# A two-layer hybrid diffusion block: six buffers for the first modulation weights, and the state space model's input without its repeated part in DRAM

## The chip, the cores and the metric

The kernel runs on one core of a Trainium2 chip. The metric is the device time of one execution in microseconds (us); less is better. A time shown for a kernel is the median of several executions; the profile is of one execution more.

## The reference, cut to what matters

Context (256 tokens) and latent (512 tokens) pass through the same two layers. Width is 1024, everything is fp32. A layer modulates the normed tokens by six vectors that come from one product of a 1024-vector with a 1024x6144 matrix, projects them once for four mixers, joins these by one output projection, and ends in a gated ConvFFN.

```python
for l in range(DEPTH):
    m = silu(c) @ ada_w + ada_b + ada_table[l]          # shift, scale, gate, twice
    h = modulate(rmsnorm(x, g0), shift1, scale1)
    p = h @ w_in[l]                                     # 256 + 768 + 1024 + 352 columns
    y = concat(s5(p), hyena(p), retention(p), mla(p)) @ w_out[l]
    x = x + gate1 * rmsnorm(y, g1)
    h = modulate(rmsnorm(x, g2), shift2, scale2)
    y = (silu(a) * v) @ w_down[l]                       # a, v: depthwise conv of h @ w_up[l]
    x = x + gate2 * rmsnorm(y, g3)

def s5(u):                       # 16 groups of 16 channels, 64 complex states each
    h_f = scan(abar_f, bbar_f @ u); h_b = scan(abar_b, bbar_b @ u reversed)
    y = gelu(Re(C_f h_f + C_b h_b) + d_skip * u)
    return y * sigmoid(y @ glu_w + glu_b)
```

The first block of modulation vectors (a 1024x2048 matrix: shift and scale of the first norm of the first layer) is needed before anything can be projected. The backward scan of the latent tokens starts from the state that the context leaves behind; this is why its input holds the context's part at both ends.

## The kernel before, in words

The work is written as generators (the mixers of a layer, preparations of tables, modulation blocks), woven together by the program and then put in one order for each engine (TensorE PE, VectorE DVE, ScalarE ACT, GpSimd POOL, and SP, which issues most transfers) by a scheduler. Each engine runs its own list in order. A product is done in three passes: a weight tile of 128x1024 (512 KB, pool names `wr` raw, `wh` and `wl`) is loaded, cast by ACT (L303) to its high part, DVE subtracts it to get the low part (L304), and PE multiplies high by high, low by high and high by low (L335, L339).

**The start** (L1676 to L1711). Three tiles of x, each of 1024 channels by 256 tokens (1 MB, two transfers, L1686), are loaded, then a loop walks the letters of `W_START`: `x` does the norm of the next x tile (`xnorm`, L1691: ACT squares L1502, PE sums them over channels L1481, a root on DVE L402 to L408, PE spreads it L423, DVE multiplies L1695), `p` runs a step of `s5_prep` (tables of the state space model), `s` a step of `hy_spectra` (the Hyena filters), and `a` a step of `ada(0)` (L463): step k loads two tiles of the modulation matrix (L473, buffer name `ar`, three buffers that every such product shares) and multiplies them by the vector (L478, four matmuls). After eight steps the row is copied (L481), transposed (L484), added to its bias (`mod`, L488) and turned into the norm's gain (`der`, L497). Then `norm_half` (L1526) scales x on ACT (L1530) and DVE (L1528) and splits it into high and low parts (`H1h`, L1531, ACT; `H1l`, L1532, DVE; H1 is the latent tokens, H0 the context). With these the in-projection of the first layer begins.

**The state space model.** `s5_in` (L957) projects its 256 input channels first and stores each half (128 channels, 8 phases j, 96 chunks n) into the DRAM tile `s5_u`, whose rows have 128 places per phase: the 96 chunks (L967) and once more the first 32, which are the context's (L968). `s5_run` (L970) loads that into a tile U with phases and channels in the partitions (L977, eight transfers, one per phase) and its kernel T (L978, eight transfers), alternating, all on POOL's queue. `states` (L981) multiplies U by the input matrices (L995: forward columns 0 to 95, backward columns 127 down to 32), DVE rotates and scans (L1002 to L1016); the outputs are L1027 to L1035. At the end u is loaded once more for the skip term (L1061). In the same queue POOL copies the roots of a retention norm (into a tile also named `A_SB`, L1235, behind a wait for DVE), starts transfers of the latent attention's operands (B_Q and B_R, L1365; `wh` and `wl` from `B_kr`, L1367) and clears A_HS (L1011), all in one list in order.

**The second layer's** in-projection comes in the order state space, Hyena, retention, MLA; the retention's values are made last by `ip_v` (L1742; weights `w_v`, matmuls L1749 to L1751), and `s5_run` and the rest are woven in behind.

Of the kernel before, what the change touches and what calls it, by code (L numbers as in the profile page):

```python
# [19 lines left out]
L = 2  # L20
# [3 lines left out]
KD = D // 128  # L24
# [3 lines left out]
NCH = NT // 8  # L28
# [12 lines left out]
QUEUES = "ssssassssp"  # L41
W_START = "xaxapxsapasapasaaa"
TLS = False
# [182 lines left out]
def tile_kernel(ctx, tc, I, out, dbg=None, upto=None):  # L226
# [9 lines left out]
    def new(p, shape, tag, dt=F32, **kw):  # L236
        return p.tile(list(shape), dt, tag=tag, name=nm(tag), **kw)
# [195 lines left out]
    def dtile(shape, tag):  # L433
        return new(dr, shape, tag)
# [7 lines left out]
    hy_Kc = dtile([2, 2, 128, 768], "hy_Kc")  # L442
    s5_u = [dtile([256, 8, 128], f"s5_u{l}") for l in range(L)]
    s5_y = [dtile([256, 8, NCH], f"s5_y{l}") for l in range(L)]
# [20 lines left out]
    def ada(b):  # L465

        md, der = mods[0]
        ps = sm_ps()
        for k in range(KD):
            raws = []  # L470
            for h in range(2):
                raw = new(wp, [128, 1024], "ar", bufs=3)
                qa.dma_start(raw, I["ada_w"][b, k, h])  # L473
                raws.append(raw)
            for h in range(2):
                for j in range(2):
                    q = 32 * (2 * h + j)
                    pe.matmul(ps[q:q + 32], c2[:, k], raws[h][:, j * 512:(j + 1) * 512], start=(k == 0), stop=(k == KD - 1))  # L478
            yield
        row = new(wp, [128, 512], "ar", bufs=3)  # L480
# [478 lines left out]
    def s5_in(l, inproj):  # L959
        for i in range(2):  # L960
# [4 lines left out]
            act.copy(tv[:, 0:32], o[0].rearrange("p (n j) -> p n j", j=8))  # L965
            u = s5_u[l][128 * i:128 * i + 128]
            qs.dma_start(u[:, :, 0:96], t)  # L967
            qs.dma_start(u[:, :, 96:128], t[:, :, 0:32])  # L968

    def s5_run(l, p, put, segs, busy=lambda: False):  # L970
        ud, yd = s5_u[l].rearrange("(g c) j n -> j c g n", c=16), s5_y[l].rearrange("(g c) j n -> j c g n", c=16)
        n0 = 0 if 0 in segs else 32
# [3 lines left out]
        for j in range(8):  # L976
            qp.dma_start(U[16 * j:16 * j + 16], ud[j])  # L977
            qp.dma_start(T[16 * j:16 * j + 16].rearrange("c g (i x) -> c g i x", i=8), s5_T[l][:, :, j:j + 8, :])  # L978
        tt = dve.tensor_tensor

# [77 lines left out]
        for i in range(2):  # L1058
            tu = new(p, [128, 2, 8, NCH], ("A_U", "A_T")[i])
            t, u = tu[:, 0], tu[:, 1]  # L1060
            qc.dma_start(u[:, :, n0:], s5_u[l][128 * i:128 * i + 128][:, :, n0:96])  # L1061
            qc.dma_start(t[:, :, n0:], s5_y[l][128 * i:128 * i + 128][:, :, n0:])
# [552 lines left out]
    for l in range(L):  # L1615
# [48 lines left out]
        with ExitStack() as base, ExitStack() as esl, ExitStack() as esr:  # L1664
# [5 lines left out]
            if l == 0:  # L1670
# [9 lines left out]
                with mkpool("start", side="right") as px:  # L1680
                    g0 = ada(0)
                    X = []
                    for i, (s, h) in enumerate(subs):
# [4 lines left out]
                        if i == 0:  # L1688
                            c2 = ada_setup()

                    def xnorm(x):  # L1691
# [337 lines left out]
```

## Time and profile before

| | us |
|---|---|
| median of 3 runs | 2100.9 (2097.35 to 2101.09) |
| the profiled execution | 2094.68 |
| its span, from the first to the last instruction | 2092.9 |

| engine | busy us | share of the span |
|---|---|---|
| PE, matmuls | 1917.5 | 92% |
| PE, weight loads | 1563.2 | 75% |
| DVE | 1350.6 | 65% |
| ACT | 796.8 | 38% |
| POOL | 136.8 | 7% |

The mean granted clock of PE is 0.948 of full speed. The span has these parts: the start (0 to 68.9 us), the first layer's in-projection with the tables woven in (to 340), its mixers and output projection (to 600), its ConvFFN (to 1345, with the second layer's in-projection behind it to about 1430), the mixers of the second layer (to 1720) and the last ConvFFN. A stretch in which PE is busy for less than its length is one where something else ends last.

### The profile page before, as it was taken

To read this page: it belongs to the slowest core of one execution; us is meant where nothing else is said; L and a number is where in the kernel's file an instruction comes from. 1 tells how busy PE (TensorE), PEld (TensorE's weight loads), DVE (VectorE), ACT (ScalarE), POOL (GpSimd) and SP (SyncE) were. 2 spreads that over 40 slices of the span, in tenths; PEclk is the share of its full clock that TensorE was granted. 3 is DMA by queue.
4 is the path that set the end of the run, shared out by engine and by line. 5 is a ranking of instruction groups with operands and counts; after the bars stand their busy time and mean duration, and the time that the engine had idled before them with its cause. 6 is when DMAs were issued, how large, how long until landed. Compare 5 with 4: busy or idle time off the path is not lost. (4 is left out here: it accounts for less than half of the span.)

```text
span 2092.9 us, 29826 instructions
## 1 busy us (share of the span) xinstructions
PE 1917.5 (92%) x11318; PEld 1563.2 (75%) x11318; DVE 1350.6 (65%) x2850; ACT 796.8 (38%) x1355; POOL 136.8 (7%) x158
## 2 busy tenths in 40 slices
PE   5899899787899799899999999889989989999996
PEld 1677676566688678788888888678867878888885
DVE  5777474686746897876856445738877455555555
ACT  3656222343334332343533233423355434333332
POOL 0121002100001000110000000110021000000000
PEclk7899999789999899999999999899989989999998
DMA  7566446625442468234133222395631424232231
GB/s 254 178 215 219 172 147 195 155 78 165 149 163 91 154 208 283 92 104 143 59 97 139 86 63 69 104 227 170 219 106 53 137 74 132 92 100 96 96 101 41
DMA packets 147127, 283.96 MB, mean 136 GB/s; under 512 B 35397, under 2 KB 78566, under 8 KB 146984
## 3 DMA queue, kind: packets, MB, share of 16 engines
q1 hardware_dynamic: 139304, 273.65, 40.5%
q0 software_dynamic: 3072, 7.08, 2.0%
q10 hardware_dynamic: 4608, 1.31, 0.3%
q8 instruction: 90, 1.47, 0.3%
q14 instruction: 53, 0.43, 0.1%
HBM read 230.12 MB, written 48.99 MB: 133 GB/s over the span
## 5 line engine op out<-in xcount | busy, mean ns | idle before, releaser
L304 DVE TENSOR_TENSOR wl<-wr,wh 128x1024 fp32r<-128x1024 f32 x174 | 213.3, 1228 | 277.7 <-ACT wh L303 273.9
L339 PE MATMUL mm<-H1h,wh 128*128 128x512 f32 x888 | 355.9, 401 | 14.4 <-DVE st L430 13.4
L339 PE MATMUL mm<-H1l,wh 128*128 128x512 f32 x888 | 353.9, 399 | 0.0
L339 PE MATMUL mm<-H1h,wl 128*128 128x512 f32 x888 | 353.4, 398 | 0.3 <-DVE wl L304 0.3
L303 ACT CAST wh<-wr 128x1024 fp32r<-128x1024 f32 x174 | 182.1, 1050 | 353.1 <-PE mm L339 288.0
L339 PEld LDWEIGHTS mm<-H1h,wh 128*128 128x128 f32 x888 | 169.1, 190 | 59.0 <-issue 17.0
L339 PEld LDWEIGHTS mm<-H1l,wh 128*128 128x128 f32 x888 | 169.4, 191 | 39.0 <-issue 3.2
L339 PEld LDWEIGHTS mm<-H1h,wl 128*128 128x128 f32 x888 | 169.0, 190 | 39.1 <-issue 2.0
L339 PE MATMUL mm<-H0h,wh 128*128 128x256 f32 x480 | 137.6, 287 | 9.6 <-DVE st L430 8.4
L339 PE MATMUL mm<-ff_mh,wh 128*128 128x512 f32 (+1 forms) x432 | 135.0, 363 | 8.4 <-DVE st L430 3.6
L339 PE MATMUL mm<-H0h,wl 128*128 128x256 f32 x480 | 137.2, 286 | 0.0
L339 PE MATMUL mm<-H0l,wh 128*128 128x256 f32 x480 | 136.9, 285 | 0.0
L339 PE MATMUL mm<-ff_ml,wh 128*128 128x512 f32 (+1 forms) x432 | 133.2, 359 | 0.0
L339 PE MATMUL mm<-ff_mh,wl 128*128 128x512 f32 (+1 forms) x432 | 132.8, 359 | 0.0
L339 PEld LDWEIGHTS mm<-H0h,wh 128*128 128x128 f32 x480 | 92.2, 192 | 17.3 <-issue 14.5
L339 PEld LDWEIGHTS mm<-H0h,wl 128*128 128x128 f32 x480 | 92.0, 192 | 4.6 <-issue 4.4
L339 PEld LDWEIGHTS mm<-H0l,wh 128*128 128x128 f32 x480 | 91.9, 192 | 3.2 <-issue 2.4
L1549 POOL TENSOR_TENSOR x<-x,y 128x512 f32<-128x512 f32 x20 | 28.4, 1426 | 994.6 <-ACT n_sq L1995 368.5
L1936 DVE TENSOR_TENSOR y<-mm,y 128x512 f32<-128x512 f32 x80 | 53.3, 686 | 59.4 <-PE mm L339 59.4
L339 PEld LDWEIGHTS mm<-ff_mh,wh 128*128 128x128 f32 x432 | 73.4, 192 | 23.6 <-DVE y L1936 5.1
L428 ACT ACTIVATE st<-mm,c_ffn_v 128x512 f32<-128x512 f32 (+1 forms) x132 | 88.6, 702 | 4.6 <-PE mm L354 4.6
L429 DVE SCALAR_TENSOR_TENSOR st<-mm,c_ffn_v,st 128x511 f32<-128x511 f32 (+1 forms) x132 | 83.4, 653 | 3.5 <-ACT st L428 3.5
(610 smaller groups left out, 4192.8 us busy)
## 6 DMA issues: line engine op xcount, KB each, us to landing
wr<-in_w_up SPq DMA_DIRECT2D x88, 512.0 KB, 3.6
ar<-in_ada_w SPq DMA_DIRECT2D x48, 512.0 KB, 4.6
ar<-in_ada_t SPq DMA_DIRECT2D x48, 512.0 KB, 4.4
wr<-in_w_down SPq DMA_DIRECT2D x44, 512.0 KB, 3.4
wr<-in_w_in SPq DMA_DIRECT2D x34, 512.0 KB, 4.5
ar<-in_k_tabl SPq DMA_DIRECT2D x16, 512.0 KB, 4.0
wr<-in_w_out SPq DMA_DIRECT2D x16, 512.0 KB, 4.6
xs_d<-x SPq DMA_DIRECT2D x8, 1024.0 KB, 5.0
```

Source lines behind the costliest of these rows:

```text
L303: act.copy(hi, raw)
L304: dve.tensor_tensor(lo, raw, hi.bitcast(F32), ALU.subtract)
L339: pe.matmul(outs[s], w, X(k, s, j), start=f, stop=z)
L428: act.activation(u[:, o:o + m], ps, AF.Identity, bias=vw[:, 3:4], scale=vw[:, 1:2])
L429: dve.scalar_tensor_tensor(u[:, o + 1:o + m], ps[:, 0:m - 1], vw[:, 0:1], u[:, o + 1:o + m], ALU.mult, ALU.add)
L1549: (pool, dve)[k // 2 % 2].tensor_tensor(x[:, ks], x[:, ks], y[:, ks], ALU.add)
L1936: dve.tensor_tensor(d, ps, d, ALU.add)
```

## The change

Four things are changed.

- `ada(0)` no longer shares three buffers: its two tiles of each step go to an `ar` and a `wr` buffer, three of each. Steps 0 to 2 are loaded when the first `run(g0, 1)` is made, which is behind the first x tile; each later step loads the tiles of the step three ahead. The later blocks of `ada` are as before.
- `W_START` has one `p` and one `s` less (these steps run later, in the in-projection), and `a` stands where they stood.
- `s5_u` holds 96 chunks per phase, with no repeated part; one transfer stores it, 3072 B in one piece per partition, where there were pieces of 384 B and 128 B. U is loaded into the first 96 columns in pieces of 384 B (512 B before), and POOL copies columns 0 to 31 to 96 to 127. The last reload of u takes the whole row.
- In `s5_run` the eight transfers of T are issued first, then the eight of U.

```diff
--- before.py
+++ after.py
@@ -39,7 +39,7 @@
 REUSE = "pool"
 
 QUEUES = "ssssassssp"
-W_START = "xaxapxsapasapasaaa"
+W_START = "xaxaxapasapasaaa"
 TLS = False
 W_FF = 1
 N_OPEN = (3, 3)
@@ -440,7 +440,7 @@
     s5_rot = [dtile([2, 4, 128, 576], f"s5_rot{l}") for l in range(L)]
     hy_K = [dtile([4, 2, 128, 768], f"hy_K{l}") for l in range(L)]
     hy_Kc = dtile([2, 2, 128, 768], "hy_Kc")
-    s5_u = [dtile([256, 8, 128], f"s5_u{l}") for l in range(L)]
+    s5_u = [dtile([256, 8, NCH], f"s5_u{l}") for l in range(L)]
     s5_y = [dtile([256, 8, NCH], f"s5_y{l}") for l in range(L)]
     cat_d = [[dtile([128, NT], f"cat{l}_{i}") for i in range(8)] for l in range(L)]
     pd = [[dtile([128, NT], f"pd{l}_{i}") for i in range(19)] for l in range(L)]
@@ -466,16 +466,26 @@
 
         md, der = mods[0]
         ps = sm_ps()
-        for k in range(KD):
+        def load(k):
             raws = []
             for h in range(2):
-                raw = new(wp, [128, 1024], "ar", bufs=3)
+                raw = new(wp, [128, 1024], "wr" if early and h else "ar", bufs=3)
                 qa.dma_start(raw, I["ada_w"][b, k, h])
                 raws.append(raw)
+            return raws
+
+        early, ahead = b == 0, []
+        if early:
+            ahead = [load(k) for k in range(3)]
+            yield
+        for k in range(KD):
+            raws = ahead.pop(0) if early else load(k)
             for h in range(2):
                 for j in range(2):
                     q = 32 * (2 * h + j)
                     pe.matmul(ps[q:q + 32], c2[:, k], raws[h][:, j * 512:(j + 1) * 512], start=(k == 0), stop=(k == KD - 1))
+            if early and k + 3 < KD:
+                ahead.append(load(k + 3))
             yield
         row = new(wp, [128, 512], "ar", bufs=3)
         act.copy(row, ps)
@@ -963,9 +973,7 @@
             tv = t.rearrange("p j n -> p n j")
             act.copy(tv[:, 32:96], o[1].rearrange("p (n j) -> p n j", j=8))
             act.copy(tv[:, 0:32], o[0].rearrange("p (n j) -> p n j", j=8))
-            u = s5_u[l][128 * i:128 * i + 128]
-            qs.dma_start(u[:, :, 0:96], t)
-            qs.dma_start(u[:, :, 96:128], t[:, :, 0:32])
+            qs.dma_start(s5_u[l][128 * i:128 * i + 128], t)
 
     def s5_run(l, p, put, segs, busy=lambda: False):
         ud, yd = s5_u[l].rearrange("(g c) j n -> j c g n", c=16), s5_y[l].rearrange("(g c) j n -> j c g n", c=16)
@@ -974,8 +982,10 @@
         U = new(p, [128, 16, 128], "A_U")
         T = new(p, [128, 16, 128], "A_T")
         for j in range(8):
-            qp.dma_start(U[16 * j:16 * j + 16], ud[j])
             qp.dma_start(T[16 * j:16 * j + 16].rearrange("c g (i x) -> c g i x", i=8), s5_T[l][:, :, j:j + 8, :])
+        for j in range(8):
+            qp.dma_start(U[16 * j:16 * j + 16, :, 0:NCH], ud[j])
+        pool.tensor_copy(U[:, :, NCH:128], U[:, :, 0:128 - NCH])
         tt = dve.tensor_tensor
 
         def states(qt, d):
@@ -1058,7 +1068,7 @@
         for i in range(2):
             tu = new(p, [128, 2, 8, NCH], ("A_U", "A_T")[i])
             t, u = tu[:, 0], tu[:, 1]
-            qc.dma_start(u[:, :, n0:], s5_u[l][128 * i:128 * i + 128][:, :, n0:96])
+            qc.dma_start(u, s5_u[l][128 * i:128 * i + 128])
             qc.dma_start(t[:, :, n0:], s5_y[l][128 * i:128 * i + 128][:, :, n0:])
             dve.scalar_tensor_tensor(t[:, :, n0:], u[:, :, n0:], vec256[:, l, 0, i:i + 1], t[:, :, n0:], ALU.mult, ALU.add)
             act.activation(t[:, :, n0:], t[:, :, n0:], AF.Gelu_apprx_tanh)
@@ -1687,6 +1697,7 @@
                         X.append(x)
                         if i == 0:
                             c2 = ada_setup()
+                            run(g0, 1)
 
                     def xnorm(x):
                         t = [new(px, [128, 2, 256], "t", bufs=2) for _ in range(4)]
```

Lines of the kernel after are 10 or 11 higher behind the first of these places.

**SP at the start.** The transfers behind the constants, before (`wr` is a weight tile of the in-projection, `x` one of x):

```order
L452 DMA c_c_188<-in_c 128x16
L1686 DMA x_199<-in_x 128x4x256
L299 DMA wr_595<-in_w_in 128x1024
L1686 DMA x_199<-in_x 128x4x256
L1686 DMA x_202<-in_x 128x4x256 x2
L473 DMA ar_248<-in_ada_w 128x1024
L473 DMA ar_250<-in_ada_w 128x1024
L473 DMA ar_298<-in_ada_w 128x1024
L299 DMA wr_680<-in_w_in 128x1024
L473 DMA ar_300<-in_ada_w 128x1024
L555 DMA q_lam_306<-in_s_A 128x96
```

and now:

```order
L452 DMA c_c_188<-in_c 128x16
L473 DMA ar_200<-in_ada_w 128x1024
L473 DMA wr_202<-in_ada_w 128x1024
L473 DMA ar_204<-in_ada_w 128x1024
L473 DMA wr_206<-in_ada_w 128x1024
L473 DMA ar_208<-in_ada_w 128x1024
L473 DMA wr_210<-in_ada_w 128x1024
L1696 DMA x_212<-in_x 128x4x256 x2
L1696 DMA x_215<-in_x 128x4x256 x2
L473 DMA ar_264<-in_ada_w 128x1024
L473 DMA wr_266<-in_ada_w 128x1024
```

Six tiles of the modulation matrix stand ahead of the second and third x tile, and the first in-projection weights stand behind all sixteen (further down, out of this piece).

**DVE at the start**, around the first modulation vectors, now (`y_kk` is a step of the Hyena filters, `wl` a low part of an in-projection weight):

```order
L304 TENSOR_TENSOR wl_654<-wr_651,wh_653 128x1024
L609 TENSOR_SCALAR q_co_439<-q_co_439,c_k_sgn_70 128x32
L758 TENSOR_SCALAR y_kk_465<-y_kk_465 64x256
L498 TENSOR_TENSOR mod_85_162<-sm_484,c_ada_b_85 128x4x4
L760 SCALAR_TENSOR_TENSOR y_kk_465<-y_kk_465 64x256
L498 TENSOR_TENSOR mod_85_162<-sm_484,c_ada_b_85 128x4x4
L760 SCALAR_TENSOR_TENSOR y_kk_465<-y_kk_465 64x256
L507 SCALAR_TENSOR_TENSOR der_86_163<-mod_85_162,c_norm_g_84 128x16
L304 TENSOR_TENSOR wl_894<-wr_891,wh_893 128x1024
L760 SCALAR_TENSOR_TENSOR y_kk_465<-y_kk_465 64x256
L1538 TENSOR_SCALAR x_183<-x_183,der_86_163,mod_85_162 128x256
L761 TENSOR_SCALAR y_kk_465<-y_kk_465 64x256
```

Behind these come the other scalings of x and the first H1l. Two of the three low parts of weights stand ahead of `mod` and the third behind `der`; before, two were done long ahead of it, between the norms of x, and the third stood behind H1l.

**POOL in the first layer**, around the copy of the retention's roots into A_SB, before:

```order
L1235 COPY A_SB_3447<-rq_y_3433 128x256
L978 DMA A_T_3534<-s_T_18_95 16x16x128
L977 DMA A_U_3533<-s_u_25_102 16x16x128
L978 DMA A_T_3534<-s_T_18_95 16x16x128
L977 DMA A_U_3533<-s_u_25_102 16x16x128
L978 DMA A_T_3534<-s_T_18_95 16x16x128
L977 DMA A_U_3533<-s_u_25_102 16x16x128
L978 DMA A_T_3534<-s_T_18_95 16x16x128
L1011 MEMSET A_HS_3567 128x4
L1367 DMA wh_4000<-B_kr_2938 32x768
L1367 DMA wl_4001<-B_kr_2938 32x768
```

and now:

```order
L1245 COPY A_SB_3445<-rq_y_3431 128x256
L985 DMA A_T_3532<-s_T_18_95 16x16x128 x8
L987 DMA A_U_3531<-s_u_25_102 16x16x96 x4
L1021 MEMSET A_HS_3566 128x4
L1377 DMA wh_3999<-B_kr_2936 32x768
L1377 DMA wl_4000<-B_kr_2936 32x768
L988 COPY A_U_3531<-A_U_3531 128x16x32
```

Of the sixteen transfers of U and T seven stood behind the copy into A_SB, and twelve do now, with the copy inside A_U behind them and behind two for the latent attention.

**PE in the second layer**, around the first state matmuls (A_SB here is the state space model's input matrix), before:

```order
L1751 MATMUL mm_12995<-wh_12963,H0l_11096 128x256
L1749 MATMUL mm_12995<-wh_12963,H0h_11095 128x256
L1750 MATMUL mm_12995<-wl_12964,H0h_11095 128x256
L1751 MATMUL mm_12995<-wh_12963,H0l_11096 128x256
L995 MATMUL sm_12015<-A_U_11991,A_SB_12009 64x96 x8
L995 MATMUL sm_12045<-A_U_11991,A_SB_12039 64x96 x8
L1749 MATMUL mm_12995<-wh_12963,H0h_11095 128x256
```

and now:

```order
L339 MATMUL mm_13159<-H1h_11092,wh_13155 128x512
L339 MATMUL mm_13159<-H1l_11093,wh_13155 128x512
L339 MATMUL mm_13159<-H1h_11092,wl_13156 128x512
L1005 MATMUL sm_12013<-A_U_11988,A_SB_12007 64x96 x8
L1005 MATMUL sm_12043<-A_U_11988,A_SB_12037 64x96 x8
L1037 MATMUL sm_12072<-A_U_11988,A_T_11989 128x64
L339 MATMUL mm_13159<-H1h_11092,wh_13155 128x512
```

The state matmuls stood in the midst of the values' matmuls (L1749 to L1751; L1760 to L1762 now), and now stand behind all of them and behind the first 18 of the next weight tile's.

## Rows read from the trace of the kernel before

**Rows 1.** Busy time by stretch: length; each engine; PE clock, DMA share, GB/s.
```profile
68.90:340.00 271.10, 260.30 (x1507) 197.28 (x1507) 179.44 (x407) 117.11 (x208) 34.22 (x28) 0.97 0.56 184
...
1345.00:1430.00 85.00, 71.16 (x435) 61.87 (x435) 40.53 (x78) 27.11 (x44) 9.22 (x19) 0.90 0.76 192
...
1430.00:1540.00 110.00, 107.90 (x638) 92.63 (x637) 91.77 (x209) 41.48 (x69) 6.88 (x11) 0.98 0.59 188
```

**Rows 2.** Windows of the start.
```profile
0.00:20.00 20.00, 6.09 (x28) 2.04 (x32) 6.13 (x26) 7.65 (x11) 0.21 (x4) 0.80 0.85 283
...
20.00:40.00 20.00, 16.33 (x74) 5.05 (x68) 13.80 (x58) 9.72 (x16) 0.00 (x0) 0.67 0.67 215
...
15.00:20.00 5.00, 1.62 (x6) 0.47 (x10) 1.65 (x2) 0.00 (x0) 0.00 (x0) 0.50 1.05 397
```

**Rows 3.** Waits 0 to 110: engine, tile, line <- releaser: us, times, longest.
```profile
PE sm L478 <- DMA ar<-in_ada_w: 11.5, 5, 5.3
```

**Rows 4.** Timeline of PE at the start: start, us, line, operation [idle before].
```profile
57.27 1.05 PE L478 MATMUL sm<-ar,ada_c 128*32 128x512 f32 x4 [1.01 <-DMA ar<-in_ada_w]
...
60.80 1.11 PE L484 MATMUL sm<-c_k_ident,ar 128*128 128x128 f32 x4
...
68.91 0.58 PE L335 MATMUL mm<-H1l,wh 128*128 128x256 f32 x1 [3.49 <-DVE H1l L1532]
```

**Rows 5.** Timeline of DVE at the start.
```profile
34.31 1.21 DVE L550 TENSOR_TENSOR q_tp<-q_tp,q_PB 128x1024 f32<-128x1024 f32 x1
...
38.48 2.35 DVE L1695 TENSOR_TENSOR x<-x,sm 128x1024 f32<-128x1024 f32 x2 [0.84 <-PE sm L423]
...
61.95 0.27 DVE L488 TENSOR_TENSOR mod<-sm,c_ada_b 128x16 f32<-128x16 f32 x2 [0.35 <-PE sm L484]
...
67.64 2.36 DVE L1532 TENSOR_TENSOR H1l<-x,H1h 128x1024 fp32r<-128x1024 f32 x2
...
76.06 1.22 DVE L304 TENSOR_TENSOR wl<-wr,wh 128x1024 fp32r<-128x1024 f32 x1
```

**Rows 6.** Timeline of ACT at the start.
```profile
45.00 0.42 ACT L752 ACTIVATE y_win<-y_kk 64x256 f32<-64x256 f32 x1 [8.38 <-DVE y_kk L751]
```

**Rows 7.** Timeline of POOL, first layer.
```profile
388.09 0.40 POOL L1235 COPY A_SB<-rq_y 128x256 f32<-128x256 f32 x1 [8.11 <-DVE rq_y L408]
```

**Rows 8.** Window before the first states.
```profile
398.00:400.00 2.00, 0.00 (x0) 0.00 (x0) 0.00 (x0) 0.00 (x0) 0.00 (x0) 0.50 1.27 102
```

**Rows 9.** Timeline of PE, first layer: the first state matmuls.
```profile
401.03 1.55 PE L995 MATMUL sm<-A_U,A_SB 128*64 128x96 f32 x16 [5.14 <-DMA wh<-B_kr]
```

**Rows 10.** Window in the second layer.
```profile
1360.00:1364.00 4.00, 3.54 (x25) 2.88 (x24) 2.88 (x4) 2.21 (x4) 0.00 (x0) 1.00 1.04 176
```

**Rows 11.** Timeline of ACT, second layer.
```profile
1398.79 1.04 ACT L303 CAST wh<-wr 128x1024 fp32r<-128x1024 f32 x1 [10.87 <-DMA wr<-in_w_v]
```

**Rows 12.** Timeline of PE before and after the stall.
```profile
1375.40 0.39 PE L339 MATMUL mm<-H1l,wh 128*128 128x512 f32 x1
...
1375.63 0.39 PE L339 MATMUL mm<-H1h,wl 128*128 128x512 f32 x1
...
1402.68 0.55 PE L339 MATMUL mm<-H0h,wh 128*128 128x256 f32 x1 [8.44 <-DVE st L430]
...
1403.03 0.63 PE L339 MATMUL mm<-H1l,wh 128*128 128x512 f32 x1
...
1403.68 0.63 PE L339 MATMUL mm<-H1h,wl 128*128 128x512 f32 x1
```

**Rows 13.** Timeline of PE: values, first states, and the later mixer chain.
```profile
1413.50 0.28 PE L1750 MATMUL mm<-wl,H0h 128*128 128x256 f32 x1
...
1413.62 0.28 PE L1751 MATMUL mm<-wh,H0l 128*128 128x256 f32 x1
...
1418.86 1.54 PE L995 MATMUL sm<-A_U,A_SB 128*64 128x96 f32 x32
...
1538.24 2.76 PE L1302 MATMUL sm<-wr,st 128*128 128x256 f32 x12
```

## The prediction, made before the change was run

> **What bounds the kernel now.** I read the windows by stretch first. In the first layer's in-projection PE is busy 260.3 of 271.1 us at a granted clock of 0.97, so there the work itself ends last; towards the end of the second layer's in-projection it is 71.16 of 85 at 0.90, then 107.9 of 110 [rows 1]. The start is far from that: PE works 6.09 us in the first 20 and 16.33 in the next 20, while the transfers have a DMA share of 0.85 and 0.67 [rows 2]. The list of waits says for whom PE stands there: 11.5 us in 5 waits at the modulation product L478 for its tiles [rows 3]. In the timeline the last four matmuls L478 begin at 57.27, behind a wait for their tile; the transposes of the row follow at 60.80, and the in-projection's stream at 68.91, behind 3.49 us for H1l, so 11.64 us lie between last tile and stream [rows 4]. So the kernel has some idle time at the start, some before each state space model, and little elsewhere. Below I go through these three places. The sum is against the profiled execution's own 2094.68 us, which is 6.2 under the median of the runs shown, 2100.9; the forecast puts the difference on the median.
>
> **The start.** Six buffers let SP issue the sixteen tiles of 512 KB without waiting for the product. At 397 GB/s, the rate of the window from 15 to 20 us [rows 2], a tile takes 524288 B / 397 GB/s = 1.32 us. The order of SP now has constants, six tiles, four halves of x (also 512 KB each), and ten tiles: with the first x and the constants, 1.4 MB, ahead of them (5 us at the 283 GB/s of the first 20 us [rows 2], and 4 more until it flows and for small pieces, an estimate), the twenty end at 9 + 20 x 1.32 = 35.4, and small loads and later weights among them make it about 39. **By the loads alone** the stream would begin at 39 + 11.64 = 50.6, so 18.3 us earlier than 68.91 [rows 4]. I do not take that, since DVE and ACT have lists of their own. Before, the last norm product on DVE began at 38.48 and took 2.35 [rows 5]. Its x tile now comes behind six tiles of the modulation, but its squares on ACT no longer stand behind matmuls L478 that wait; I put its end at 36.7 instead of 40.8 (some 4 us, an estimate from rows 5 and the waits of rows 3). In DVE's order some 28 steps of the state space tables now stand behind it, which ran ahead of it before: the last of them takes 1.21 [rows 5], the small ones 0.1 to 0.2, in all about 6.0, so 42.7. Then comes the sine of the Hyena filters: ACT's y_win, which closes it, began 4.2 us behind that norm [rows 6, 5], so 46.9 now, 0.42 for itself; the matmul that reads y_win stands just ahead of the transposes in PE's list, so these are at about 49. With their 1.1 us [rows 4] and two low parts of weights at 1.22 each [rows 5] in DVE's list ahead of `mod`, which had been done long before, `mod` comes at 52.6, where it was at 61.95. From `mod` to the stream were 6.96 us [rows 5, 4]; the H1l steps now stand behind six scalings of x, not twelve and two table steps, which saves about 3.3, and the third low part costs 1.2: 4.9. The stream begins at about 57.6: **-11** (bounds -7, if nothing but the waits for tiles goes, of 11.5 us [rows 3] with some given back, and -18.3).
>
> The `p` and `s` steps that left the loop, some 6.7 us of DVE work, run under the in-projection, where DVE is busy 179.44 of 271.1 us [rows 1]: hidden, save that low parts of weights come behind them in places; I take **+1** (0 to +3). If the cover went, it would be all 6.7.
>
> **The first layer's state space model.** Here the order of POOL speaks against the change. The copy into A_SB at 388.09 waits 8.11 us for DVE, and everything behind it in POOL's list waits too; the first state matmuls begin at 401.03 after 5.14 us of idle PE [rows 7, 9]. The row names a transfer of `wh`; but U and T, issued behind the copy, were still landing: from 398 to 400 the queues are full (share 1.27) and move 102 GB/s [rows 8]. One transfer of U or T is 16x16x128 words = 131 KB: 1.28 us of all engines at that rate. Before, seven stood behind the copy, 9.0 us; now eight T and four U of 98 KB (0.96 us each), 10.3 + 3.9 = 14.1 us, and the copy within U. Its duration is in no row; the nearest is the copy of 128x256 in 0.40 [rows 7], twice its words here, so 0.4 to 0.8. PE needs U alone, but the change puts U last. The difference is 5.1 + 0.6; as some of this lands while the copy's other followers are issued, I take **+5** (0, if other waits end later anyway; +9, if all twelve start only when the queue is clear).
>
> What the row shows is that pieces of 512 B are slow already. The Trainium skill, DMA: Bandwidth & Descriptors, section Specifications, gives 512 B as the smallest transfer for the full rate, with a read-modify-write below. By that the four U loads of 384 B pieces would cost about double, another 3.9 us, so +9 for this place; no row of U at 384 B exists, and the trace agrees only in so far as 512 B pieces move at a quarter of the 397 GB/s.
>
> **The second layer's.** Here the stores count. From 1360 on the queues are full at 176 GB/s [rows 10]; the weights of `w_v` come late, ACT waits 10.87 us for them and casts at 1398.79, PE stands 8.44 us until 1402.68 and then runs at half clock: L339 takes 0.63 where it took 0.39; a step of the 128x512 form and one of the 128x256 form together are 0.65 apart (1403.03 to 1403.68) where 0.23 and about 0.12 were enough [rows 12, 13]; eight such pairs follow, 2.4 us lost [rows 11, 12]. The change takes transfers away: a store of 524 KB at 176 GB/s is 3.0 us, of 393 KB in pieces of 3072 B at about 390 GB/s 1.0: 2 us each, 4 for both; U is 262 KB less, 1.5 us. So the stall gets 5.5 shorter, and the lost clock with it: -7.9. Against that stands PE's order. The first state matmuls, at 1418.86, stood among the values' matmuls that are 0.12 apart [rows 13]; now 102 of these and 18 of L339 (0.23 apart [rows 12]) come ahead, 12.2 + 4.1 = 16.3 us. The same work is done, but this filler is missing behind, where the attention's values at 1538.24 [rows 13] end a chain of DVE steps that the filler covered (107.9 of 110 us busy [rows 1]). If all is exposed: +16.3; if none: 0. Neither end has a nearer row; I take half, +8. Sum **0** (-8 to +8).
>
> The whole reload of u, two transfers in a contiguous piece, lies beside other work in both layers: nothing. In-projection of the first layer hides its own stores.
>
> **Sum:** -11 + 1 + 5 + 0 = -5: 2089.7 for the profiled execution, 2096 for the median of runs, or -0.24%. Its own range is 2090 to 2103.
>
> **The rivals.**
> 1. *The loads alone decide the start, and the second layer's stall goes without an exposed chain.* For it: PE's waits there name the tiles [rows 3], and DVE is busy 6.13 of the first 20 us and 13.80 of the next [rows 2]. Against: the lists above. -18 + 1 + 5 - 8 = -20: 2081.
> 2. *The start gives it back:* `mod` waits for DVE's low parts and the third norm, so that only -6 is left: -6 + 1 + 5 + 0 = 0: 2101. The same result if the loads are not early at all: SP's order says that they are issued early, yet they could just share the 397 GB/s with x and delay its norm.
> 3. *Slower: U arrives behind T.* The states of both layers come later than their PE filler lasts: +9 in the first (all twelve transfers behind a full queue), +16.3 - 7.9 = +8.4 in the second, with -10 from the start and 1: +8, 2109. It decides from the point at which the two exposures (17 us) are more than what the start gains (10 to 11). For it: PE stands 5.14 us at the first states already, with full queues.
>
> **Chances.** Forecast 0.40, loads alone 0.22, given back 0.18, slower 0.20. A measurement of this kernel can tell about 0.2%, 4.2 us, from no change: 2096.7 to 2105.1. The forecast's own range splits 0.25 faster, 0.13 same, 0.02 slower; the first rival is all faster; the second 0.03, 0.12, 0.03; the third 0.03 same and 0.17 slower. Faster 0.50, same 0.28, slower 0.22. The range reaches from the middle of the first rival, 2079, to the third, 2109.
>
> **What would show it.** Right: the in-projection's stream begins near 57 to 58 us, the last L486 near 40 with no long waits for tiles, and `mod` later than the tiles would ask; the first states of layer one 4 to 6 us later against the copy into A_SB, PE idle about 10 us before them; the stall at `w_v` about 3 us; more idle PE near the attention's values. Wrong: a stream at 51 (the loads decide), or at 64 (DVE decides more); states as early as before; a stall of 8 us that stays, which would say that the stores weren't what the queue was full of.

## The result and the profile after

The changed kernel takes 2114.22 us (median of 4 runs, 2111.59 to 2115.40), the kernel before 2099.12 (4 runs): a ratio of 1.0081, 95% interval 1.0063 to 1.0098. So it is 15 us slower, where 2096 and a range up to 2109 had been forecast. Its profiled execution took 2115.22 us with a span of 2113.4, which is 20.5 us more than the span before; the granted clock of PE is 0.947, before it was 0.948. The execution that was profiled before (2094.68) lies 4.4 us under its median and the one after 1.0 above its own, so 5.4 of the 20.5 us belong to the two executions and not to the change.

The start went as forecast. PE's timeline of the changed kernel there (start, us, engine, line, operation, and in brackets the idle time before it and what ended it):

```profile
42.21 1.05 PE L486 MATMUL sm<-wr,ada_c 128*32 128x512 f32 x4 [0.28 <-DMA wr<-in_ada_w]
...
49.46 1.11 PE L494 MATMUL sm<-c_k_ident,ar 128*128 128x128 f32 x4
...
57.52 0.58 PE L335 MATMUL mm<-H1h,wh 128*128 128x256 f32 x1 [6.95 <-ACT H1h L1541]
58.82 0.58 PE L335 MATMUL mm<-H1l,wh 128*128 128x256 f32 x1 [0.71 <-DVE H1l L1542]
```

Against [rows 4] the last modulation matmuls are 15.06 us earlier, the transposes 11.34, the stream 10.09. So the tiles no longer decide (0.28 us of wait); ACT and DVE do, since the 6.95 us ahead of the stream are a wait for H1h. DVE's timeline behind the transposes shows the two low parts ahead of `mod` and the third ahead of the scaling:

```profile
50.03 1.21 DVE L304 TENSOR_TENSOR wl<-wr,wh 128x1024 fp32r<-128x1024 f32 x1
...
51.47 1.21 DVE L304 TENSOR_TENSOR wl<-wr,wh 128x1024 fp32r<-128x1024 f32 x1
...
52.95 0.17 DVE L498 TENSOR_TENSOR mod<-sm,c_ada_b 128x16 f32<-128x16 f32 x1
...
53.94 1.21 DVE L304 TENSOR_TENSOR wl<-wr,wh 128x1024 fp32r<-128x1024 f32 x1
...
57.55 2.35 DVE L1542 TENSOR_TENSOR H1l<-x,H1h 128x1024 fp32r<-128x1024 f32 x2
```

But the 10 us are gone by the copy into A_SB in the first layer, and POOL and PE lose more behind it (POOL's and PE's timelines of the changed kernel):

```profile
388.17 0.40 POOL L1245 COPY A_SB<-rq_y 128x256 f32<-128x256 f32 x1 [8.60 <-DVE rq_y L408]
388.69 4.47 POOL L985 DMA_DIRECT2D A_T<-s_T  x8
...
404.96 0.61 POOL L988 COPY A_U<-A_U 128x512 f32<-128x512 f32 x1 [3.46 <-DMA A_U<-s_u]
```

```profile
405.06 1.55 PE L1005 MATMUL sm<-A_U,A_SB 128*64 128x96 f32 x16 [6.10 <-DMA A_U<-s_u]
```

The copy stands at 388.17 where it stood at 388.09 [rows 7], and the first states 4.03 us later than before [rows 9]. In the second layer PE's timeline has the shorter stall, the states behind the values, and then a new wait:

```profile
1403.50 0.36 PE L339 MATMUL mm<-H0h,wh 128*128 128x256 f32 x1 [2.88 <-DVE st L430]
...
1434.71 1.54 PE L1005 MATMUL sm<-A_U,A_SB 128*64 128x96 f32 x32
...
1551.58 1.97 PE L423 MATMUL sm<-c_k_ident,rq_y 128*128 128x128 f32 x8 [9.50 <-DVE rq_y L408]
1553.34 3.01 PE L1312 MATMUL sm<-wr,st 128*128 128x256 f32 x11
```

The stall of 8.44 us [rows 12] is 2.88 now, and the values' matmuls begin at 1413.24 where they began at 1413.38: at that point the changed kernel is where the one before was. The attention's values come 15.1 us later than in [rows 13], behind 9.50 us of wait for the roots of a norm. The windows say the same: between 1345 and 1430 PE is busier than in [rows 1], between 1430 and 1540 less, and then comes a hole:

```profile
1345.00:1430.00 85.00, 75.48 (x437) 64.74 (x437) 34.90 (x60) 33.39 (x56) 10.99 (x20) 0.94 0.65 185
1430.00:1540.00 110.00, 102.87 (x641) 87.64 (x639) 91.42 (x211) 36.59 (x57) 1.03 (x8) 0.97 0.63 200
1530.00:1560.00 30.00, 16.64 (x69) 12.90 (x67) 17.30 (x40) 10.80 (x22) 9.82 (x12) 0.66 0.29 83
```

### The profile page after: what moved, and what is told of

The parts are those of the page before. It is cut to its first block, busy times and chain, and to the rows that moved or that the text cites. A ratio compares the mean times of both kernels' runs of the same rounds, so it can differ in the third digit from the quotient of the medians.

```text
span 2113.4 us, 29808 instructions
## 1 busy us (share of the span) xinstructions
PE 1920.9 (91%) x11318; PEld 1567.6 (74%) x11318; DVE 1364.0 (65%) x2850; ACT 794.1 (38%) x1353; POOL 138.4 (7%) x160
## 3 DMA queue, kind: packets, MB, share of 16 engines
q0 software_dynamic: 3072, 6.56, 1.7%
q10 hardware_dynamic: 4608, 1.31, 0.3%
## 5 line engine op out<-in xcount | busy, mean ns | idle before, releaser
L429 DVE SCALAR_TENSOR_TENSOR st<-mm,c_ffn_v,st 128x511 f32<-128x511 f32 (+1 forms) x132 | 83.5, 654 | 3.5 <-ACT st L428 3.5
```

The lines of the kernel that those rows point to most:

```text
L429: dve.scalar_tensor_tensor(u[:, o + 1:o + m], ps[:, 0:m - 1], vw[:, 0:1], u[:, o + 1:o + m], ALU.mult, ALU.add)
```

## The experiments

Twelve kernels were run, each beside the kernel before on the same chip. The table gives the lead or lag against the profiled execution before at five places of PE's timeline, in us (minus is earlier; taken from the starts of the same instructions in each trace): the in-projection's stream, the last transposes of the retention roots L1239 in the first layer (they read A_SB), that layer's first states, the values' first matmul in the second layer, and the last group of L1444, with which that layer's mixers end. All of it is measured against one trace of the kernel before; the account of the prediction below shows that this trace is quick in the stretch ahead of the last column.

| kernel | measured ratio (95%) | stream | L1239 | states | values 2 | mixers 2 |
|---|---|---|---|---|---|---|
| changed kernel | 1.0081 (1.0063 to 1.0098) | -10.1 | 0.0 | +4.0 | -0.1 | +19.5 |
| 1 start only | 0.9982 (0.9968 to 0.9995) | -11.4 | -12.8 | -10.4 | -8.8 | 0.0 |
| 2 S5 part only | 1.0031 (1.0017 to 1.0045) | +1.6 | -0.7 | -2.0 | -11.0 | +8.0 |
| 3 S5 part, by turns | 1.0018 (1.0003 to 1.0032) | -1.9 | -5.7 | -7.0 | -10.2 | +6.1 |
| 4 T first only | 1.0032 (1.0019 to 1.0045) | -0.6 | -2.9 | -3.8 | -3.8 | +6.2 |
| 5 start, S5 by turns | 1.0087 (1.0068 to 1.0106) | -11.0 | -1.1 | +5.0 | +1.7 | +17.0 |
| 6 start, T first | 0.9995 (0.9982 to 1.0007) | -10.0 | -10.8 | -8.5 | -13.5 | -1.2 |
| 7 all, U first | 0.9981 (0.9966 to 0.9995) | -10.3 | +1.6 | -0.6 | -14.5 | -4.3 |
| 8 start, U first, old input | 0.9952 (0.9933 to 0.9971) | -10.7 | -11.6 | -19.6 | -20.0 | -12.6 |
| 9 changed, second store | 1.0016 (1.0002 to 1.0030) | -11.5 | -9.5 | -7.4 | -15.8 | +3.0 |
| 10 U first, second store | 0.9916 (0.9899 to 0.9932) | -11.5 | -10.2 | -18.3 | -24.7 | -13.9 |
| 11 U first only | 1.0010 (0.9996 to 1.0025) | -1.7 | -6.2 | -13.2 | -4.5 | +4.2 |
| 12 as 10, store read | 1.0022 (1.0005 to 1.0039) | -11.5 | -9.7 | -17.8 | -16.0 | +7.0 |

### The parts alone

The first question was which part loses the time. Kernel 1 has the six buffers, the early loads and the new `W_START` in the kernel before:

```diff
-W_START = "xaxapxsapasapasaaa"
+W_START = "xaxaxapasapasaaa"
...
+                            run(g0, 1)
...
+            ahead = [load(k) for k in range(3)]
```

> Only the start is changed (six buffers for the first modulation block, its early loads, two letters less in W_START); the state space model's input, its loads and their order are those of before, and so is the second layer's order on PE. Theory 'deferred': the stream begins about 10 us earlier, and the table steps that left the start take it back before the first layer's states (in the changed kernel the lead is 10.1 us at 58.8 and 0 at the copy into A_SB, 388.6): same as before within 3 us, about 2099. Theory 'start holds': the lead was lost only because of the state space model's part, so 9 to 10 us faster, about 2089.

Measured: 2093.09 us against 2095.77, -0.18%. The lead was not taken back before the first states: it is 12.8 us at L1239. So 'deferred' falls in its place (the table steps under the in-projection cost nothing that shows), and 'start holds' in its size: against the one trace before, the lead is gone in the second layer, where 8.8 us at the values become 0.0 at the end of the mixers. In this kernel PE also waits 14.15 us for U in the first layer, of which more below.

Kernel 2 has the state space model's part alone, kernel 3 the same with U and T loaded by turns, kernel 4 only T ahead of U:

```diff
-            qp.dma_start(U[16 * j:16 * j + 16], ud[j])
             qp.dma_start(T[16 * j:16 * j + 16].rearrange("c g (i x) -> c g i x", i=8), s5_T[l][:, :, j:j + 8, :])
+        for j in range(8):
+            qp.dma_start(U[16 * j:16 * j + 16], ud[j])
```

> Only the state space model's part is changed (input without its repeated part, copy on chip, T loaded first); the start is that of before. Theory 'deferred': this part carries the whole loss: +5 us at the first layer's states, -6 at the stall for the values' weights, +15 to +20 from the states that stand behind all of the values' matmuls in the second layer, so +15 to +19, about 2116. Theory 'start holds': it must then carry +25, about 2124.

> As the run before, but U and T are loaded by turns as in the kernel before; only the storing without the repeated part and the copy on chip remain. In PE's list of the second layer all of the values' matmuls still stand ahead of the first states (the 18 of the next weight tile do not). Theory 'copy': the second layer's loss comes with the copy's place in the plan, not with T first, so this loses most of what the run before lost: +8 to +14 (the first layer's +5 goes). Theory 'T first': the order of the loads is what delays the states: within 4 us of before or faster, by the shorter stall.

> Only the order of the loads is changed (T, then U); the input keeps its repeated part, nothing is copied. In PE's list of the second layer 71 of the values' 144 matmuls stand ahead of the states, where before 45 did. Theory 'copy': +3 to +7, from the first layer's states alone (twelve of sixteen transfers behind the copy into A_SB) and 3 us of moved filler. Theory 'T first': +12 or more, as much as the run with the whole state space part.

Measured: +0.31%, +0.18% and +0.32%, so 6.5, 3.8 and 6.7 us. Both theories asked for far more of kernel 2; kernel 3 is just within the 4 us that 'T first' allowed, and far under what 'copy' asked; kernel 4 lies at the upper edge of 'copy'. So neither 'copy' nor 'T first' holds in both of the kernels it was asked of. What follows is in the sum: start and S5 part together would be +0.13%, and the changed kernel has +0.81%. Some 14 us are in neither part. Place by place: in the first layer the start alone leads by 12.8 at L1239, the S5 part alone by 0.7, both together by 0.0. In the second layer kernels 2 and 3 lose 19.0 and 16.3 us between the values and the end of the mixers, the changed kernel 19.6. Not all of this belongs to the S5 part: the kernels with the old input (1, 4, 6, 8 and 11) lose 7.4 to 12.3 us there too.

### Which pair

Kernel 5 is the changed kernel with U and T by turns, kernel 6 the new start with T first and the old input (the loads of kernel 4).

> The whole change except that U and T are loaded by turns, as before. By the sum of the single parts (start -0.18%, input without its repeated part +0.18%) it would be 0.0%, about 2096. The first runs' parts did not add up to the changed kernel (+0.13% by their sum, +0.81% measured); theory 'pair': the start and the input without its repeated part spoil each other through the plan of the first layer, whatever the order of the loads: +0.5% to +0.8%, 2106 to 2113. Theory 'T first': the order of the loads is what turns the start's lead into nothing: 0.0% here.

> The new start with T loaded ahead of U; the input keeps its repeated part and nothing is copied on chip. By the sum of the single parts (-0.18% and +0.32%) +0.14%, about 2099. Theory 'pair': as this sum, since the input is the old one. Theory 'T first': +0.5% or more, about 2107.

Measured: +0.87% and -0.05%. 'Pair' has the right side in both, though kernel 5 is slower than its band and kernel 6 faster than its sum: the new start and the input without its repeated part spoil each other, and the lead at L1239 is gone whatever the order of the loads (0.0, -1.1 and +1.6 us in the changed kernel and kernels 5 and 7). The place is in the first layer, in the list of PE's waits from 300 to 400 us. The changed kernel:

```profile
PE sm L423 <- DVE rq_y L408: 5.0, 1, 5.0
```

Kernel 5 has 5.2 in the same place, kernel 7 has 5.4; kernels 1, 6, 8 and 9 have no such wait in that list. L423 spreads the roots of the latent attention's norms, which DVE computes in steps L402 to L408. DVE's timeline of the changed kernel there, and PE's matmul that waits:

```profile
327.25 0.17 DVE L402 TENSOR_SCALAR rq_v<-sm 128x6 f32<-128x6 f32 x1 [4.11 <-PE sm L417]
...
331.80 0.75 DVE L429 SCALAR_TENSOR_TENSOR st<-mm,c_hy_v,st 128x511 f32<-128x511 f32 x1 [2.70 <-ACT st L428]
...
332.61 0.74 DVE L430 SCALAR_TENSOR_TENSOR st<-mm,c_hy_v,st 128x511 f32<-128x511 f32 x1
333.27 0.15 DVE L408 SCALAR_TENSOR_TENSOR rq_y<-rq_a,rq_y 128x4 f32<-128x4 f32 x1
...
334.50 1.70 DVE L406 TENSOR_TENSOR rq_a<-rq_y 128x4 f32<-128x4 f32 x1
...
336.59 1.46 DVE L407 SCALAR_TENSOR_TENSOR rq_a<-rq_a,rq_v 128x4 f32<-128x4 f32 x1
...
338.45 1.47 DVE L408 SCALAR_TENSOR_TENSOR rq_y<-rq_a,rq_y 128x4 f32<-128x4 f32 x1
...
340.03 1.77 DVE L408 SCALAR_TENSOR_TENSOR rq_y<-rq_a,rq_y 128x6 f32<-128x6 f32 x1
...
342.24 0.38 DVE L408 SCALAR_TENSOR_TENSOR rq_y<-rq_a,rq_y 128x6 f32<-128x6 f32 x1
```

```profile
342.76 2.36 PE L423 MATMUL sm<-c_k_ident,rq_y 128*128 128x128 f32 x10 [5.02 <-DVE rq_y L408]
```

and of kernel 1:

```profile
325.51 0.16 DVE L402 TENSOR_SCALAR rq_v<-sm 128x6 f32<-128x6 f32 x1 [3.18 <-PE sm L417]
...
327.49 0.17 DVE L408 SCALAR_TENSOR_TENSOR rq_y<-rq_a,rq_y 128x4 f32<-128x4 f32 x1
...
329.35 1.69 DVE L406 TENSOR_TENSOR rq_a<-rq_y 128x4 f32<-128x4 f32 x1
...
331.55 0.17 DVE L408 SCALAR_TENSOR_TENSOR rq_y<-rq_a,rq_y 128x6 f32<-128x6 f32 x1
...
332.76 0.75 DVE L429 SCALAR_TENSOR_TENSOR st<-mm,c_hy_v,st 128x511 f32<-128x511 f32 x1 [1.04 <-ACT st L428]
```

```profile
331.87 1.27 PE L423 MATMUL sm<-c_k_ident,rq_y 128*128 128x128 f32 x10
```

In kernel 1 two steps of the key's rotation stand between the roots, and the Hyena convolution's steps (L429, L430) come behind; in the changed kernel the convolution's steps stand between too. From the second L402 to the last L408 the chain takes 6.0 us in kernel 1 and 15.0 in the changed kernel. The 9 us more have two parts. The first L429 waits 2.70 us for ACT, and the four steps of the convolution take 2.4. The rest is in root steps of 1.46 to 1.77 us where most take 0.16: there are four in the changed kernel and one in kernel 1. They end with POOL's products of the retention's states (L1184), which share no tile with them. POOL's timeline of the changed kernel, and of kernel 1:

```profile
334.12 7.66 POOL L1184 TENSOR_TENSOR A_HS<-A_GT,A_T 64x768 f32<-64x768 f32 x4
```

```profile
328.98 2.04 POOL L1184 TENSOR_TENSOR A_HS<-A_GT,A_T 64x768 f32<-64x768 f32 x1
```

In the fourteen traces 53 root steps take 0.8 us or more, and each ends 0.02 to 0.03 us behind the end of one of POOL's TENSOR_TENSOR instructions; of the 5638 short ones (under 0.3 us) none lies within such an instruction. So a root step that meets one of these waits for its end. A chain of small steps becomes hostage to another mixer's steps on its own engine and on POOL: the last root comes 10.7 us later than in kernel 1, L423 10.9 us later, and L1239 12.8. PE itself stands only 5.02 us of this; it is the chain through DVE and POOL to A_SB and U that is late. The comparison is with kernel 1, since the kernel before has another order here (its L423 begins at 334.28).

### U ahead of T

Kernel 7 is the changed kernel with U loaded first and copied at once; kernel 8 the new start with the old input and U first.

```diff
         for j in range(8):
+            qp.dma_start(U[16 * j:16 * j + 16, :, 0:NCH], ud[j])
+        pool.tensor_copy(U[:, :, NCH:128], U[:, :, 0:128 - NCH])
+        for j in range(8):
             qp.dma_start(T[16 * j:16 * j + 16].rearrange("c g (i x) -> c g i x", i=8), s5_T[l][:, :, j:j + 8, :])
-        for j in range(8):
-            qp.dma_start(U[16 * j:16 * j + 16, :, 0:NCH], ud[j])
-        pool.tensor_copy(U[:, :, NCH:128], U[:, :, 0:128 - NCH])
```

> The whole change, but U is loaded ahead of T and copied as soon as it is there. In PE's list of the second layer 71 of the values' 144 matmuls stand ahead of the first states (in the changed kernel all 144). Theory 'states late': the states' place behind the values' matmuls is what exposes 15 us in the second layer, so this is 8 to 12 us faster than the changed kernel's +0.81%: about +0.3%, 2102. Theory 'fixed latency': the second layer's end is set by chains of DVE steps that do not care where the states stand; then +0.7% stays, 2110.

> The new start, the input with its repeated part as before, U loaded ahead of T. In the second layer's list the first states stand ahead of all of the values' matmuls (0 of 144; before 45). Theory 'states late': the second layer takes 6 to 10 us less than in the run with the new start alone, whose lead of 8.8 us at the values' matmuls was all gone at the end of the mixers: -0.5% to -0.7%, 2081 to 2085. Theory 'fixed latency': as the new start alone, -0.2%, 2092.

Measured: -0.19% and -0.48%. Kernel 7 is 21 us better than the changed kernel (1.0081 to 0.9981), more than 'states late' asked; the number of kernel 8 lies just outside its forecast, and not for the reason given: its second layer loses 7.4 us from the values to the mixers' end, little less than kernel 1's 8.8, and the gain is the first layer's states, 19.6 us early instead of 10.4. With T first or by turns PE waits long for U there, with U first much less (kernel 1, then kernel 9, then kernel 10, all with the new start):

```profile
390.63 1.55 PE L1005 MATMUL sm<-A_U,A_SB 128*64 128x96 f32 x16 [14.15 <-DMA A_U<-s_u]
```

```profile
393.62 1.55 PE L1007 MATMUL sm<-A_U,A_SB 128*64 128x96 f32 x16 [13.87 <-DMA A_U<-s_u]
```

```profile
382.68 1.55 PE L1007 MATMUL sm<-A_U,A_SB 128*64 128x96 f32 x16 [3.60 <-DMA A_U<-s_u]
```

### The plan, by an added store

If the place of the root steps is what counts, and not the bytes of the input, then something that only moves them must give the time back. Kernel 9 is the changed kernel with one unread store more; kernel 10 adds the same to kernel 7:

```diff
+    s5_w = [dtile([256, 8, 32], f"s5_w{l}") for l in range(L)]
...
             qs.dma_start(s5_u[l][128 * i:128 * i + 128], t)
+            qs.dma_start(s5_w[l][128 * i:128 * i + 128], t[:, :, 0:32])
```

> The changed kernel with one thing added: the context's part is stored once more, into a DRAM tile of its own that nobody reads (so more work, not less). In DVE's list of the first layer the attention norm's root steps (L402 to L408) then stand together again, with the Hyena convolution's two steps (L429, L430) behind them as in the run with the new start alone, and not between them as in the changed kernel; in the second layer all 144 of the values' matmuls still stand ahead of the states. Theory 'plan': the roots' place is what took the start's lead, so the copy into A_SB of the first layer comes at 376 to 379 and not at 388, and the time is 9 to 12 us under the changed kernel's: +0.25% to +0.4%, 2102 to 2105. Theory 'pieces': the input without its repeated part costs by its transfers, so this is as slow as the changed kernel or slower: +0.8% or more, 2114.

> The whole change with U ahead of T (71 of 144 matmuls ahead of the second layer's states) and the same unread store added. Theory 'plan': 8 to 12 us under the same kernel without that store, which had -0.19%: -0.6% to -0.75%, 2081 to 2085, as good as the new start with U first and the old input, or a little better by the shorter stall for the values' weights. Theory 'pieces': -0.1% to -0.2%, 2093.

> The kernel before with U loaded ahead of T and nothing else. In the second layer the states stand ahead of all of the values' matmuls. Theory 'states late': the gain of the same order of loads beside the new start (from -0.18% to -0.48%) is its own: -0.3%, 2091. If the second layer's end is instead fixed by what happens in front of it, no change, 2097.

Measured: 9 takes 2101.23 us, +0.16% instead of +0.81%, with L1239 9.5 us ahead and the copy into A_SB at 377.31: 'plan' holds and 'pieces' doesn't, since work was added and some 14 us went. Its chain of roots takes 6.0 us again, as in kernel 1:

```profile
328.43 0.16 DVE L402 TENSOR_SCALAR rq_v<-sm 128x6 f32<-128x6 f32 x1 [3.17 <-PE sm L417]
...
334.47 0.17 DVE L408 SCALAR_TENSOR_TENSOR rq_y<-rq_a,rq_y 128x6 f32<-128x6 f32 x1
```

The added store also moves POOL's products: one instead of four stands ahead of the chain's end. What the place on DVE's list is worth without that was not tried alone. Kernel 10 takes 2080.34 against 2098.09, ratio 0.9916 (0.9899 to 0.9932): it beats both kernels (by 17 us the one before), and does what 'plan' asked and a little more. Kernel 11, U first in the kernel before, was forecast at -0.3% and measured +0.10%, within its interval of no change: 13.2 us of lead at the first states are a lag of 4.2 at the end of the second layer's mixers. So 'states late' was wrong there: with the states ahead of all the values' matmuls that layer needs as long from the values to the end of the mixers as in kernel 1 (229.6 and 229.7 us).

### The second layer's wait

What then loses 15 to 20 us in the second layer against the trace before, or 7 to 12 against the kernels with the old input? The list of PE's waits from 1340 to 1580 has one line that goes with it, L423 behind the attention's roots again. The changed kernel:

```profile
PE sm L423 <- DVE rq_y L408: 15.8, 3, 9.5
...
PE mm L339 <- DVE st L430: 2.9, 1, 2.9
```

Kernels 2 and 9 have the same 15.8; 3 and 5 have 13.7, 12 has 12.8, 7 has 9.5 and 10 has 6.4. Of those with the old input, 4 has 10.8, 6 has 7.8, 11 has 6.2, 1 and 8 have 3.3 and 3.2, the kernel before 4.7. The six with 12.8 or more need 236 to 244 us from the values to the end of the mixers, the other eight 221 to 233; within each group the line doesn't sort them. The second line, the stall for the values' weights, goes the other way: 5.2 to 10.3 with the old input, at most 4.1 with the short one. DVE's timeline of the changed kernel:

```profile
1544.35 0.16 DVE L408 SCALAR_TENSOR_TENSOR rq_y<-rq_a,rq_y 128x4 f32<-128x4 f32 x1
1544.55 0.69 DVE L1318 TENSOR_TENSOR B_o<-B_P,ar 32x512 f32<-32x512 f32 x1
1545.26 1.11 DVE L406 TENSOR_TENSOR rq_a<-rq_y 128x4 f32<-128x4 f32 x1
1546.41 0.68 DVE L1319 TENSOR_TENSOR B_P<-B_P,B_o 32x512 f32<-32x512 f32 x1
1547.12 1.11 DVE L407 SCALAR_TENSOR_TENSOR rq_a<-rq_a,rq_v 128x4 f32<-128x4 f32 x1
...
1548.76 1.22 DVE L408 SCALAR_TENSOR_TENSOR rq_y<-rq_a,rq_y 128x4 f32<-128x4 f32 x1
```

and of kernel 10, where the roots begin in one piece and the key's rotation (L1318 above) has been done before, but for its last step:

```profile
1514.60 0.16 DVE L402 TENSOR_SCALAR rq_v<-sm 128x4 f32<-128x4 f32 x1 [0.75 <-PE sm L417]
...
1515.59 0.16 DVE L408 SCALAR_TENSOR_TENSOR rq_y<-rq_a,rq_y 128x4 f32<-128x4 f32 x1
...
1518.30 0.16 DVE L408 SCALAR_TENSOR_TENSOR rq_y<-rq_a,rq_y 128x4 f32<-128x4 f32 x1
```

From L402 to the last L408 this chain takes 9.3 us in the changed kernel and 3.7 in kernel 10. The four long root steps (1.1 to 1.2 us each) make up some 4 of the 5.6 us between them, the rotation's and the retention's steps the rest. POOL's products L1184 again run beside the long ones, and in kernel 10 come only behind the chain:

```profile
1544.57 6.74 POOL L1184 TENSOR_TENSOR A_HS<-A_GT,A_T 64x512 f32<-64x512 f32 x4 [12.69 <-ACT A_T L1148]
```

```profile
1519.23 5.61 POOL L1186 TENSOR_TENSOR A_HS<-A_GT,A_T 64x512 f32<-64x512 f32 x4 [0.73 <-ACT A_T L1150]
```

Kernel 12 is the rival to "the states' place decides": 71 of the 144 values' matmuls ahead, as in 10, but the wrapped columns loaded from the second store instead of copied.

```diff
-        pool.tensor_copy(U[:, :, NCH:128], U[:, :, 0:128 - NCH])
+        for j in range(8):
+            qp.dma_start(U[16 * j:16 * j + 16, :, NCH:128], s5_w[l].rearrange("(g c) j n -> j c g n", c=16)[j])
```

> As the run with U first and the second store, but that store is now read: the wrapped columns of U come by eight small transfers from its tile (128 B pieces) and POOL copies nothing. In the second layer 71 of 144 matmuls stand ahead of the states, as there. If the copy on chip is worth something of its own: eight transfers more ahead of the first states, each 33 KB, at the 100 GB/s of full queues 2.6 us in all, so -0.65% to -0.75%, 2084. If transfers of this size hide and the copy is the longer path: the same -0.84% or a little better, 2079.

Measured: +0.22%, a miss on both counts, 22 us behind kernel 10. Its first states are as early as there (-17.8); it is 7 us behind kernel 10 by the end of the first layer's attention, 8.7 us behind at the values, and 12 more go between these and the end of the second layer's mixers, where it has the changed kernel's wait once more:

```profile
1539.22 1.97 PE L423 MATMUL sm<-c_k_ident,rq_y 128*128 128x128 f32 x8 [9.50 <-DVE rq_y L408]
```

with the rotation's steps between the roots and POOL's products beside them as in the changed kernel (9.2 us from L402 to the last L408). So the number of values' matmuls ahead of the states does not decide; the wait goes with the roots' place in DVE's list and POOL's products. No run changes these alone, and what makes up the rest of the second layer's loss is open.

## Why the prediction was wrong, point by point

- **The start, -11:** right. -10.1 at the stream; transposes forecast at 49, found at 49.46, `mod` at 52.6, found at 52.95. The last tiles came later than forecast, L486 at 42.21 and not near 40, but they do not decide, as the loads alone (rival 1) would have it.
- **The deferred table steps, +1:** this is the step that failed first, and not by its own subject: the table steps cost nothing that shows (kernel 1 leads by 12.8 us at L1239), but in the changed kernel the lead was lost there all the same, 10.1 us, to a chain that the sum has no term for: the attention's roots, 15.0 us where kernels 1 and 9 need 6.0. The prediction took it that beyond the moved steps the in-projection stays as it was. That is wrong for a program whose scheduler plans every engine anew: one store fewer moved Hyena's convolution between another mixer's roots, and POOL's products beside them.
- **The first layer's states, +5:** right as far as it goes: +4.0 at the states, +5.8 by the last L1444. The wait for U is 6.10 us, where about 10 was forecast, and the copy inside U took 0.61, in the 0.4 to 0.8 given. What it missed is what lies on the other side: the new start makes U the limit even in the old order (14.15 us of wait in kernel 1), and U first is worth about 9 us there (states at -19.6 in kernel 8, -10.4 in kernel 1).
- **The second layer, -7.9 and +8:** the first term is right: stall 2.88 for the 3 forecast, and the lag of 7.0 us at the end of the ConvFFN is -0.1 at the values. The second, +8, is the other step that failed. It was a half taken between 0 and 16.3, and against the one trace before it measured the whole: +15.2 from the values' first matmul to L1312, 19.6 to the end of the mixers (7 to 12 against the kernels with the old input). Its filler is not what was lost: kernel 12 has half of the values' matmuls ahead of the states, as kernel 10, and the changed kernel's wait all the same. The end of the chain was named rightly (a chain of DVE steps in front of the attention's values); of the 15.2 us, 11.1 are waits of L423 for the roots (9.50 and 3.28, where 1.68 stood before). A small slip beside it: 99 of the values' matmuls moved ahead, not 102, since 45 of the 144 stood there before.
- **Rival 3** had the sign, and 2109 for 2114, by luck in good part. It said +9 and +8.4; measured are +4.0 at the states and +19.6 less 7.1. It kept the start's -10, which was gone by the copy into A_SB, and its U behind T is a part only: kernel 5 has U and T by turns and is as slow.
- **The doubling of 384 B pieces** does not show. It was an estimate from the Trainium skill, DMA: Bandwidth & Descriptors, section Specifications, which gives 512 B as the smallest transfer for the full rate, with a read-modify-write below. The first two transfers of U land 3.2 us after their issue in kernel 9 (384 B pieces, 96 KB) and 4.5 us in kernel 1 (512 B, 128 KB), at the median of the two. With U first PE waits 3.60 us for U of 384 B pieces and a copy in kernel 10, and 3.8 (put down to issue) for 512 B pieces in kernel 8, at the same place.

**What stays open.** Behind the first layer, kernel 1 and the kernel before issue the same instructions in the same order on every engine; still the lead of 8.8 us at the values is 0.0 at the end of the mixers. In pieces: a matmul L886 (L876 before) waits 1.73 us instead of 0.25, an L423 3.26 instead of 1.68, and the twelve L1312 (L1302 before) behind it take 4.76 us at a granted clock of 0.57 instead of 2.76 at 1.00; an L417 further on waits 2.46 instead of 1.31. All five kernels with the old input need 228 to 233 us from the values to the end of the mixers, the profiled execution before 220.9, and from the first L1302 to that end all thirteen other traces need 97.8 to 100.4 us, this one 96.0. With its time 4.4 us under its median, this speaks for a quick execution, and then the last column of the table overstates every loss by some us; but there is one trace of the kernel before, and an earlier arrival that meets the transfers less well is not ruled out.

## What to carry to other kernels

Where a scheduler orders the engines, compare the order of every in-order list near the waits that end late, also far from the edit: one store less cost here some 14 us. Keep a chain of tiny steps that a large product waits for free of steps that themselves wait for PE, and look at what POOL runs beside it. Before a loss is put down to a stretch, compare the stretch with more traces than one of the kernel before. Load first what the first matmul reads.

## What the runs showed that was not expected

An unread store made the kernel 14 us faster (1.0081 to 1.0016), which no count of bytes explains. And a DVE step of 128x4 elements, mostly 0.16 us, is shown with 1.1 to 1.8 us where one of POOL's products runs beside it, and then ends with it (all 53 such steps in fourteen traces). Steps of another chain between the roots do not lengthen them: in the changed kernel the roots from 1542.45 to 1543.45 stand between steps L1146 and take 0.15 to 0.16 us. Other DVE steps do run inside POOL's products, so this is shown for the root steps alone.
